# Retention's sample rows through a DRAM scratch, spreads by transposes, and a re-paced first norm

## The chip, the cores and the metric

The kernel runs on one core of a Trainium2 chip. Its engines are TensorE (PE, with PEld for its weight loads), VectorE (DVE), ScalarE (ACT), GpSimd (POOL) and SyncE (SP), and its loads and stores run on 16 DMA engines. The metric is the device time of one execution in microseconds. A profiled execution also gives a span, from the first to the last instruction.

## The reference

One layer of a hybrid decoder step, in float32: 256 prompt tokens and 8 sample tokens (one new token for each of 8 sequences), model width 2048.

```python
xn = rmsnorm(x, norm1_g)
proj = xn @ w_in                      # 2048 x 6144: [u | v | q | k | v | g]
# mixer A: gated MLP, 8 groups, position mixing within 128 tokens
# mixer B: retention, 8 heads of 128, decay gamma_h = 1 - 2^(-5-h):
scores = einsum('bihd,bjhd->bhij', qc, kc) * decay_mask
new_state = state * chunk_decay + einsum('bjhd,bjhe->bhde', kc * k_decay, vc)
# per-head GroupNorm, swish gate
h = x + concat(out_a, out_b) @ w_out
h = h + cross_attend(rmsnorm(h, norm2_g), mk, mv, w_cq, w_co)   # 256 memory tokens, 4 heads
h = h + square(relu(rmsnorm(h, norm3_g) @ w_ff1)) @ w_ff2       # 2048 -> 8192 -> 2048
y = rmsnorm(h, final_norm_g)
```

For a sample token b retention is one step of the recurrence: the head's 128 x 128 state of that sequence becomes gamma * state + k_b v_b, and the output is q_b times the new state. The states, the memory keys and values and the normalized v rows are outputs too.

## The kernel before

Activations lie transposed, 128 features on the partitions and 264 tokens along the row: the 8 sample tokens in columns 0 to 7, then two blocks of 128 (`TOK`). Every large product is made in three matmuls: operands are split into a rounded high part and a remainder (`wh` and `wl`, `xh` and `xl`), and hi x hi, hi x lo and lo x hi are added up in PSUM (lines 155 to 157).

**The weight stream.** A weight chunk is 256 x 512, 512 KB. `emit_dma` loads it on SP's queue into one of five raw buffers `w`, six chunks ahead; `emit_hi` casts it on ACT (L1040) and `emit_lo` subtracts on DVE (L1048), three and two chunks ahead, into four buffers each. A group is 8 chunks and gives 512 output columns in four PSUM banks. Five banks (`mm`) serve these groups; three more (`ms`) serve everything small.

**The order is written by hand.** The kernel is emitted in one Python loop over the chunks, and each engine runs its own instructions in the order of emission. A group's chunk has four points, one after every six matmuls. At each point `run_point` advances work that is due: every `chain` generator that is due goes on to its next `yield`, then one of the `tasks` that are due does (at most one per point, and one per lane), then stores that are due are issued on SP. `yield n` means due again in n points; a bare `yield` means 3. So yields set where on each engine's list an instruction stands. A group's eviction is emitted at its last point.

**The first norm.** The input projection runs on the raw x times its gain, and the norm's factor is applied at the eviction. `square_x`, a chain that starts at the end of the first group (v), squares x on ACT in four pieces (L333, L337), adds them on DVE (L339 to L342), sums over the partitions with matmuls against `ones` (`column`, L273), takes the root on GpSimd and spreads the factor over all partitions (`spread`, L281, called in `tables`). `tables` multiplies it into the rotary tables. Then v's first group is multiplied by it (L349). The second group, q, needs the tables at its eviction: `ev_rope` copies each bank on ACT (`z`, L529) and multiplies it on DVE (`ra`, L530), and only then is the bank free.

**Spread.** The root comes out as a column, one value per token on the partitions. A matmul with the column, broadcast to 128 columns, as the stationary operand and the identity as the moving one gives a tile in which every partition holds the row of factors. It is used for the first norm, the memory's norm, the norms before cross-attention and before the MLP, and twice at the end.

**Retention.** Eight heads run as tasks on two lanes beside the projection groups (even heads on r0, odd on r1). For the sample tokens a head transposes 8 columns of k and of q (L99, out `tp[0:8, 256:512]`), splits them into `kq` (L596 on ACT, L597 on DVE), and for each sample token b a matmul with a selector column `sel` spreads its k and q rows over all partitions in PSUM (`bc`, L626). DVE then updates the state of b (L629) and multiplies it by q with a sum along the row (L632, out `rjk`, sum in `rs_t`). Tokens go in four pairs per head. `rs_t` is transposed into the output tile `rp`, normalized, and written back over v. State tiles and many other tiles share 26 slots of one pool; `load_state` loads a head's state and decay table two heads ahead. The gate (`ev_g`) multiplies by the result.

**Stores** stand in a queue by due time, and the first one that is not due holds those behind it.

Of the kernel before, what the change touches and what calls it, by code (L numbers as in the profile page):

```python
# [30 lines left out]
def build(tc, I, O):  # L31
    cst = tc.tile_pool(name="cst", bufs=1)
    wpool = tc.tile_pool(name="wpool", bufs=1)
    spool = tc.tile_pool(name="spool", bufs=1)
    tpool = tc.tile_pool(name="tpool", bufs=1)
    psum = tc.tile_pool(name="psum", bufs=1, space=bass.MemoryType.PSUM)
    with cst as cst, wpool as wpool, spool as spool, tpool as tpool, psum as psum:
        with tc.manual_schedule():
            _emit(tc, cst, wpool, spool, tpool, psum, I, O)


def _emit(tc, cst, wpool, spool, tpool, psum, I, O):
    nc = tc.nc
# [40 lines left out]
    gcol = cst.tile([128, 96], F32, name="gcol")  # L84
    ones = cst.tile([128, 256], F32, name="ones")
    neghalf = cst.tile([128, 4], F32, name="neghalf")
# [116 lines left out]
    def store(dst, src, delay=10):  # L203
        stores.append((now[0] + delay, dst, src))

# [7 lines left out]
    def run_point():  # L213
        for e in list(chains):
            if e[0] <= now[0] and not advance(e):
                chains.remove(e)
        used = set()
        for e in tasks:
            if e[2] is not None:
                if e[2] in used:  # L220
                    continue
                used.add(e[2])
            if e[0] <= now[0]:
                if not advance(e):
                    tasks.remove(e)
                break
        while stores and stores[0][0] <= now[0]:
            _, dst, src = stores.popleft()
            sp.dma_start(out=dst, in_=src)

# [6 lines left out]
    class Stats:  # L237
# [40 lines left out]
        def spread(self, out, tok=TOK):  # L278
            ps = misc([128, self.n], "rsb")
            for i, (c0, n) in enumerate(tok):  # L280
                pe.matmul(ps[:, c0:c0 + n], lhsT=self.col[:, i:i + 1].broadcast_to([128, 128]),  # L281
                          rhs=ident[:, 0:n], start=True, stop=True)
            if out is None:
                return ps
            act.copy(out, ps[:])
# [15 lines left out]
    open_pool("rpool")  # L301
    dve.memset(ones[:, 0:128], 1.0 / 2048)
    dve.memset(ones[:, 128:256], 1.0)
    dve.memset(neghalf[:], -0.5)
# [12 lines left out]
    def keep_warm(count):  # L317
        for _ in range(count):
            wm = bank([128, 256], "wm")
            pe.matmul(wm[:], lhsT=ones[:, 128:256], rhs=ones[:], start=True, stop=True)  # L320

# [9 lines left out]
    def square_x():  # L331
        a = slot([128, 4, T], "sqa")
        act.activation(a[:], hT[0][:], AF.Square)  # L333
        yield
        for s in range(1, 4):
            b = slot([128, 4, T], "sqb")
            act.activation(b[:], hT[s][:], AF.Square)  # L337
            yield 2
            dve.tensor_tensor(out=a[:], in0=a[:], in1=b[:], op=ALU.add)  # L339
            yield  # L340
        dve.tensor_tensor(out=a[:, 0:2, :], in0=a[:, 0:2, :], in1=a[:, 2:4, :], op=ALU.add)
        dve.tensor_tensor(out=st1.acc[:], in0=a[:, 0, :], in1=a[:, 1, :], op=ALU.add)  # L342
        yield 3
        st1.column()
        yield 4
        tables()
        for m in R4:
            vt = S["v"][0][:, m, :]
            dve.tensor_tensor(out=vt, in0=vt, in1=S["rs1"][:], op=ALU.mult)  # L349
# [6 lines left out]
    def clear():  # L356
        zt = half("zt")
        dve.memset(zt[:], 0.0)
        S["kq"] = [S["rpool"].tile([128, 256], F32R, name="kq", tag="kq", bufs=2) for _ in range(2)]
        yield  # L360
        for i in range(2):
            act.copy(S["kq"][i][:], zt[:, 0:256])
        dve.tensor_tensor(out=sel[:], in0=ident[:, 0:8], in1=ident[:, 32:40], op=ALU.add)
        act.activation(halfgn[:], gcol[:, G_GN:G_GN + 8], AF.Copy, scale=0.5)
# [125 lines left out]

    mix = {}

# [27 lines left out]
    def ev_rope(which, g):  # L520
        def ev(ps):
            o = slot([128, 4, T], which)
            S.setdefault(which, []).append(o)
            tab = S["tab"]
            ta = 0 if which == "q" else 2
            z = [t264("z") for _ in R4]
            a = [t264("ra") for _ in R4]
            for m in R4:
                act.copy(z[m][:], ps[m][:])  # L529
                dve.tensor_tensor(out=a[m][:], in0=ps[m][:], in1=tab[:, ta, :], op=ALU.mult)  # L530

            def gen():
                for m in R4:
                    for lo, hi in ((0, 64), (64, 0)):
                        gp.tensor_tensor(out=o[lo:lo + 64, m, :], in0=z[m][hi:hi + 64, :],
                                         in1=tab[hi:hi + 64, ta + 1, :], op=ALU.mult)
                yield 10
                for m in R4:
                    dve.tensor_tensor(out=o[:, m, :], in0=o[:, m, :], in1=a[m][:], op=ALU.add)
                if which == "k" and g == 0:  # L540
                    retentions(0)
            chain(gen())
            if which == "q" and g == 0:
                chain(clear(), 12)
        return ev
# [22 lines left out]
    def load_state(h):  # L568
        if h < 8:
# [4 lines left out]
            S["state"][h] = (t, d)  # L574

    def retention(h):
        g, m = h // 4, h % 4
# [3 lines left out]
        def row(name):  # L581
            return S["rpool"].tile([128, 384], F32, name=name, tag="st", bufs=4)

        kn, vn = row("kn"), row("vn")
        sm = S["rpool"].tile([128, 384], F32, name="sm", tag="sm", bufs=2)
        kq = S["kq"][h % 2]
        tp = misc([128, 512], "tp")
        for i in range(2):
            c0 = TOK[i][0]
            transpose(tp[:, i * 128:(i + 1) * 128], kt[:, c0:c0 + 128])  # L590
        for i, src in enumerate((kt, qt)):
            transpose(tp[0:8, 256 + i * 128:384 + i * 128], src[:, 0:8])
        for i in range(2):
            act.activation(kn[:, i * 128:(i + 1) * 128], tp[:, i * 128:(i + 1) * 128], AF.Copy,
                           scale=kdec[:, i * 8 + h:i * 8 + h + 1])
        act.copy(kq[0:8, :], tp[0:8, 256:512])  # L596
        dve.tensor_tensor(out=kq[32:40, :], in0=tp[0:8, 256:512], in1=kq[0:8, :].bitcast(F32), op=ALU.subtract)  # L597
        yield
        tp = misc([128, 256], "tp")
# [3 lines left out]
        act.copy(vn[:, 0:256], tp[:])  # L603
        yield
        sc = misc([128, 384], "sc")
# [4 lines left out]
        load_state(h + 2)  # L610
        yield
        pp = misc([128, 128], "pp")
# [6 lines left out]
        act.activation(st[:], st[:], AF.Copy, scale=GAMMA[h])  # L619
        yield  # L620
        rs_t = S["rpool"].tile([128, 8], F32, name="rs_t", tag="rs_t", bufs=2)
        for b0 in range(0, 8, 2):
            bc = misc([128, 2, 256], "bc")
            for j in range(2):
                b = b0 + j
                pe.matmul(bc[:, j, :], lhsT=sel[:, b:b + 1].broadcast_to([128, 128]), rhs=kq[:], start=True, stop=True)  # L626
            for j in range(2):
                b = b0 + j
                dve.scalar_tensor_tensor(out=st[:, b, :], in0=bc[:, j, 0:128], scalar=vt[:, b:b + 1],  # L629
                                         in1=st[:, b, :], op0=ALU.mult, op1=ALU.add)  # L630
                j2 = S["rpool"].tile([128, 128], F32, name="rjk", tag="rjk", bufs=1)
                dve.scalar_tensor_tensor(out=j2[:], in0=st[:, b, :], scalar=1.0, in1=bc[:, j, 128:256],  # L632
                                         op0=ALU.mult, op1=ALU.mult, accum_out=rs_t[:, b:b + 1])
            yield 2
        store(O["state_s"][h], st[:])
# [32 lines left out]
        for i, (c0, n) in enumerate(TOK):  # L668
            transpose(tp[:, c0:c0 + n], rn[0:n, i * 128:(i + 1) * 128])
        act.activation(vt, tp[:], AF.Copy, scale=halfgn[:, h:h + 1])  # L670

    def ev_g(g):
        def ev(ps):
# [3 lines left out]
            def gen():  # L677
                w = [t264("gw") for _ in R4]
                for m in R4:
                    act.activation(w[m][:], z[m][:], AF.Tanh, scale=0.5)  # L680
                yield
                for m in R4:
                    dve.scalar_tensor_tensor(out=w[m][:], in0=w[m][:], scalar=1.0, in1=z[m][:],
# [42 lines left out]
    def mem_prep():  # L726
# [15 lines left out]
        def fin():  # L742
            tok = ((0, 128), (128, 128))
            st.column(tok)
            yield 4
            S["rsmb"] = cst.tile([128, 256], F32, name="rsmb")
            st.spread(S["rsmb"][:], tok)
            S["rsm"] = st.col
# [111 lines left out]
    def ev_mk(h):  # L860
        def ev(ps):
            z = [t264("kz") for _ in R4]
            for m in R4:
                dve.tensor_tensor(out=z[m][:, 0:256], in0=ps[m][:], in1=S["rsmb"][:], op=ALU.mult)
                store(O["mem_k"][h, :, m], z[m][:, 0:256])
# [353 lines left out]
```

## Time and profile before

| | |
|---|---|
| median of 3 runs | 1600.93 us (1600.66 to 1602.39) |
| the profiled execution | 1600.87 us |
| its span | 1599.1 us |
| PE busy | 1585.5 us (99%) |
| DVE, ACT, POOL busy | 1040.9 us (65%), 751.1 us (47%), 124.1 us (8%) |
| DMA | 326.15 MB, 204 GB/s |
| granted TensorE clock | 0.999 |

In rows of the profile L155 is a line of the kernel, `acc<-xh,wh` is the tile written and those read, and a releaser behind `<-` is what ended the idle time. An f32 matmul shows as two PE records, an f32 transpose as one, and one with rounded operands as one. Busy times of matmuls overlap, since the next starts before the one ahead has drained; the distance between starts is what one costs.

### The profile page before, as it was taken

The page shows a single profiled execution, that of the slowest core. Times are in us where ns is not written, and L with a number is a line of the kernel's source. Part 1 is how long each engine was busy: PE and PEld are TensorE (multiplying, and loading weights), DVE is VectorE, ACT ScalarE, POOL GpSimd, SP SyncE. Part 2 cuts the span into 40 slices and gives each one's busy share as a digit, 9 for nine tenths or more (in the row PEclk, how much of TensorE's full clock was granted, in tenths as well). Part 3 has the DMA queues.
Part 4 walks back from the last instruction along what each step waited for, and adds up shares of the span by engine and source line. Part 5 has one row for each costly group of instructions (what it writes and reads, how often), then busy time and mean ns, then how long its engine had stood idle before and what let it go on. Part 6 is the DMA issues. An engine that isn't in the chain of part 4 may idle for free.

```text
span 1599.1 us, 31005 instructions
## 1 busy us (share of the span) xinstructions
PE 1585.5 (99%) x12608; PEld 1559.4 (98%) x12608; DVE 1040.9 (65%) x1885; ACT 751.1 (47%) x1169; POOL 124.1 (8%) x111
## 2 busy tenths in 40 slices
PE   9999999999999999999999999999999999999997
PEld 9999999999999998999999999999999999999997
DVE  6677788778658777877655555655655565565555
ACT  6455565447444444444444543534444353444443
POOL 0242022000012201010000000000000000000000
PEclk9999999999999999999999999999999999999999
DMA  8556646355578887877555555555555556555552
GB/s 291 179 208 218 217 167 198 136 196 210 188 262 287 307 301 276 294 272 250 174 183 185 183 173 186 172 190 180 177 190 172 187 172 189 180 178 187 171 188 84
DMA packets 94222, 326.15 MB, mean 204 GB/s; under 512 B 10608, under 2 KB 15728, under 8 KB 94080
## 3 DMA queue, kind: packets, MB, share of 16 engines
q1 hardware_dynamic: 94080, 324.18, 59.5%
q8 instruction: 98, 1.61, 0.4%
q14 instruction: 44, 0.36, 0.1%
HBM read 313.03 MB, written 11.11 MB: 203 GB/s over the span
## 4 chain that ended last, share of the span: by engine, by line
PE 48%; issue 46%; DVE 1%; POOL 0%; ACT 0%; POOLq 0%; DVEq 0%
PE acc L155 13%; PE acc L157 13%; PE acc L156 13%; PE acc L179 2%; PE acc L181 2%; PE acc L180 2%; PE tp L99 1%; PE qb L827 0%; PE bc L626 0%; PE spp L480 0%; PE sc L904 0%; PE op L926 0%; PE sc L903 0%; PE op L927 0%; PE pb L850 0%
## 5 line engine op out<-in xcount | busy, mean ns | idle before, releaser
L1040 ACT CAST wh<-w 128x1024 fp32r<-128x1024 f32 (+1 forms) x513 | 535.9, 1045 | 709.6 <-PE acc L156 625.4
L1048 DVE TENSOR_TENSOR wl<-w,wh 128x1024 fp32r<-128x1024 f32 (+1 forms) x513 | 628.3, 1236 | 257.2 <-ACT wh L1040 256.5
L155 PE MATMUL acc<-h2h,wh 128*128 128x264 f32 x1024 | 291.5, 285 | 0.0
L157 PE MATMUL acc<-h2h,wl 128*128 128x264 f32 x1024 | 291.1, 284 | 0.0
L156 PE MATMUL acc<-h2l,wh 128*128 128x264 f32 x1024 | 290.5, 284 | 0.0
L155 PE MATMUL acc<-rh,wh 128*128 128x264 f32 x992 | 282.2, 284 | 0.0
L157 PE MATMUL acc<-rh,wl 128*128 128x264 f32 x992 | 282.0, 284 | 0.0
L156 PE MATMUL acc<-rl,wh 128*128 128x264 f32 x992 | 281.4, 284 | 0.0
L155 PE MATMUL acc<-xh,wh 128*128 128x264 f32 x768 | 225.6, 294 | 2.8 <-DVE ra L530 2.6
L157 PE MATMUL acc<-xh,wl 128*128 128x264 f32 x768 | 219.3, 285 | 0.0
L156 PE MATMUL acc<-xl,wh 128*128 128x264 f32 x768 | 218.7, 285 | 0.0
L156 PEld LDWEIGHTS acc<-h2l,wh 128*128 128x128 f32 x1024 | 192.8, 188 | 0.0
L155 PEld LDWEIGHTS acc<-h2h,wh 128*128 128x128 f32 x1024 | 192.6, 188 | 0.0
L157 PEld LDWEIGHTS acc<-h2h,wl 128*128 128x128 f32 x1024 | 192.4, 188 | 0.0
L156 PEld LDWEIGHTS acc<-rl,wh 128*128 128x128 f32 x992 | 186.8, 188 | 0.0
L155 PEld LDWEIGHTS acc<-rh,wh 128*128 128x128 f32 x992 | 186.6, 188 | 0.0
L157 PEld LDWEIGHTS acc<-rh,wl 128*128 128x128 f32 x992 | 186.4, 188 | 0.0
L155 PEld LDWEIGHTS acc<-xh,wh 128*128 128x128 f32 x768 | 145.7, 190 | 4.9 <-DVE ra L530 3.2
L156 PEld LDWEIGHTS acc<-xl,wh 128*128 128x128 f32 x768 | 146.0, 190 | 0.2 <-DVE xl L107 0.2
L157 PEld LDWEIGHTS acc<-xh,wl 128*128 128x128 f32 x768 | 145.3, 189 | 0.0
L958 DVE TENSOR_TENSOR hT<-hT,acc 128x264 f32<-128x264 f32 x124 | 53.2, 429 | 73.2 <-PE acc L157 73.2
L95 POOL TENSOR_TENSOR msr<-msv,neghalf 128x3 f32<-128x3 f32 (+1 forms) x5 | 7.7, 1549 | 990.2 <-DVE msv L268 738.0
(253 smaller groups left out, 2777.9 us busy)
## 6 DMA issues: line engine op xcount, KB each, us to landing
w<-in_w_ff_dram SPq DMA_DIRECT2D x256, 512.0 KB, 4.1
w<-in_w_in_dram SPq DMA_DIRECT2D x95, 512.0 KB, 3.7
w<-in_w_out_dram SPq DMA_DIRECT2D x32, 512.0 KB, 4.0
w<-in_w_cq_dram SPq DMA_DIRECT2D x32, 512.0 KB, 4.2
kv<-in_kN_dram SPq DMA_DIRECT2D x32, 512.0 KB, 5.2
kv<-in_vT_dram SPq DMA_DIRECT2D x32, 512.0 KB, 4.9
w<-in_w_ck_dram SPq DMA_DIRECT2D x32, 512.0 KB, 5.6
w<-in_w_cv_dram SPq DMA_DIRECT2D x32, 512.0 KB, 4.7
```

The costliest lines, as they stand in the source:

```text
L95: gp.tensor_tensor(out=out, in0=in_, in1=neghalf[0:in_.shape[0], 0:n], op=ALU.pow)
L99: pe.transpose(out, in_, ident[0:p, 0:p])
L155: pe.matmul(ps, lhsT=a, rhs=xh, start=(i == 0), stop=False)
L156: pe.matmul(ps, lhsT=a, rhs=xl, start=False, stop=False)
L157: pe.matmul(ps, lhsT=b, rhs=xh, start=False, stop=(i == nk - 1))
L179: pe.matmul(ps, lhsT=a, rhs=hi[:, k, :], start=(kt == 0), stop=False)
L180: pe.matmul(ps, lhsT=a, rhs=lo[:, k, :], start=False, stop=False)
L181: pe.matmul(ps, lhsT=b, rhs=hi[:, k, :], start=False, stop=(kt == 15))
L958: dve.tensor_tensor(out=h[m], in0=h[m], in1=ps[m][:], op=ALU.add)
L1040: act.copy(hi[:, k, :], raws[i][:, k, :])
L1048: dve.tensor_tensor(out=lo[:, k, :], in0=raw[:, k, :], in1=hi[:, k, :].bitcast(F32), op=ALU.subtract)
```

## The change

- `sample_rows(g)`, a task once per group of four heads: copies the 8 sample columns of k and q of the four heads into one tile, transposes both (32 rows out), copies them to SBUF and stores them as 32 rows of 256 floats into a DRAM scratch `kqd{g}`.
- `rows_of(h, b0)`: a load on SP's queue of two rows (2 KB), sent to all 128 partitions, into one of four buffers `bkq`. A head asks for the first pair when it starts and for each next pair when it begins on the one before. The selector matmuls of retention, `kq` and its zeroing, split and transposes go; DVE reads `bkq` instead of PSUM and writes its throw-away product over the k half.
- Retention's yields: 2 instead of 3 between the head's first steps, 4 instead of 2 between pairs. A head waits with its start until the store of the rows has been issued.
- Stores are issued when each is due, without holding one another.
- `spread` makes transposes of the broadcast column, each 128 columns wide, the sample tokens' first so that the others overwrite what it has too much.
- `square_x` has shorter yields: squares every 2 points instead of 5, the column 6 points after the last adds instead of 3, the tables 5 points after the column instead of 4, v's products 2 points after the tables.
- `ones` has 128 columns instead of 256 and one memset fewer; the warm-up matmuls read it twice. The memory's factor moves into another pool. Cross-attention keeps its selector matmuls.

```diff
         def spread(self, out, tok=TOK):
             ps = misc([128, self.n], "rsb")
-            for i, (c0, n) in enumerate(tok):
-                pe.matmul(ps[:, c0:c0 + n], lhsT=self.col[:, i:i + 1].broadcast_to([128, 128]),
-                          rhs=ident[:, 0:n], start=True, stop=True)
+            for i, (c0, _) in reversed(list(enumerate(tok))):
+                transpose(ps[:, c0:c0 + 128], self.col[:, i:i + 1].broadcast_to([128, 128]))
...
     def square_x():
-        a = slot([128, 4, T], "sqa")
-        act.activation(a[:], hT[0][:], AF.Square)
-        yield
-        for s in range(1, 4):
-            b = slot([128, 4, T], "sqb")
+        q = []
+        for s in R4:
+            b = slot([128, 4, T], "sqa")
             act.activation(b[:], hT[s][:], AF.Square)
-            yield 2
-            dve.tensor_tensor(out=a[:], in0=a[:], in1=b[:], op=ALU.add)
-            yield
+            q.append(b)
+            yield 1
+            if s:
+                dve.tensor_tensor(out=q[0][:], in0=q[0][:], in1=q.pop()[:], op=ALU.add)
+                yield 1
+        a = q[0]
...
-        yield 3
+        yield 6
         st1.column()
-        yield 4
+        yield 5
         tables()
+        yield 2
         for m in R4:
             vt = S["v"][0][:, m, :]
             dve.tensor_tensor(out=vt, in0=vt, in1=S["rs1"][:], op=ALU.mult)
...
-                if which == "k" and g == 0:
-                    retentions(0)
+                if which == "k":
+                    defer(sample_rows(g), 2)
+                    if g == 0:
+                        retentions(0)
...
+    def sample_rows(g):
+        if g == 0:
+            S["kqd"], S["kqe"] = {}, {}
+        cols = S["rpool"].tile([128, 2, 32], F32, name="kqcol", tag="kqcol", bufs=1)
+        for i, w in enumerate("kq"):
+            act.copy(cols[:, i, :].rearrange("p (m b) -> p m b", m=4), S[w][g][:, :, 0:8])
+        yield 2
+        tp = misc([32, 2, 128], "tp")
+        for i in range(2):
+            transpose(tp[:, i, :], cols[:, i, :])
+        rows = half("kqrow")[0:32, 0:256]
+        act.copy(rows, tp[:].rearrange("p a d -> p (a d)"))
+        S["kqd"][g] = dpool.tile([32, 256], F32, name=f"kqd{g}")
+        S["kqe"][g] = store(S["kqd"][g][:], rows, 3)
+        yield
+
+    def rows_of(h, b0):
+        t = S["rpool"].tile([128, 2, 256], F32, name="bkq", tag="bkq", bufs=4)
+        r = 8 * (h % 4) + b0
+        sp.dma_start(out=t[:].rearrange("p b f -> p (b f)"),
+                     in_=S["kqd"][h // 4][r:r + 2, :].rearrange("b f -> (b f)").partition_broadcast(128))
+        return t
...
     def retention(h):
...
+        while g not in S["kqe"] or not S["kqe"][g][3]:
+            yield 2
+        yield 2
+        ahead = rows_of(h, 0)
...
-        for i, src in enumerate((kt, qt)):
-            transpose(tp[0:8, 256 + i * 128:384 + i * 128], src[:, 0:8])
...
-        act.copy(kq[0:8, :], tp[0:8, 256:512])
-        dve.tensor_tensor(out=kq[32:40, :], in0=tp[0:8, 256:512], in1=kq[0:8, :].bitcast(F32), op=ALU.subtract)
-        yield
+        yield 2
...
         for b0 in range(0, 8, 2):
-            bc = misc([128, 2, 256], "bc")
-            for j in range(2):
-                b = b0 + j
-                pe.matmul(bc[:, j, :], lhsT=sel[:, b:b + 1].broadcast_to([128, 128]), rhs=kq[:], start=True, stop=True)
+            bc = ahead
+            if b0 < 6:
+                ahead = rows_of(h, b0 + 2)
             for j in range(2):
                 b = b0 + j
                 dve.scalar_tensor_tensor(out=st[:, b, :], in0=bc[:, j, 0:128], scalar=vt[:, b:b + 1],
                                          in1=st[:, b, :], op0=ALU.mult, op1=ALU.add)
-                j2 = S["rpool"].tile([128, 128], F32, name="rjk", tag="rjk", bufs=1)
-                dve.scalar_tensor_tensor(out=j2[:], in0=st[:, b, :], scalar=1.0, in1=bc[:, j, 128:256],
+                dve.scalar_tensor_tensor(out=bc[:, j, 0:128], in0=st[:, b, :], scalar=1.0, in1=bc[:, j, 128:256],
                                          op0=ALU.mult, op1=ALU.mult, accum_out=rs_t[:, b:b + 1])
-            yield 2
+            yield 4
```

More of the change, by code (lines that the diff above doesn't have):

```diff
@@ L36, in build, with _emit @@
     psum = tc.tile_pool(name="psum", bufs=1, space=bass.MemoryType.PSUM)
-    with cst as cst, wpool as wpool, spool as spool, tpool as tpool, psum as psum:
+    dpool = tc.tile_pool(name="dpool", bufs=1, space=bass.MemoryType.DRAM)
+    with cst as cst, wpool as wpool, spool as spool, tpool as tpool, psum as psum, dpool as dpool:
         with tc.manual_schedule():
-            _emit(tc, cst, wpool, spool, tpool, psum, I, O)
-def _emit(tc, cst, wpool, spool, tpool, psum, I, O):
+            _emit(tc, cst, wpool, spool, tpool, psum, dpool, I, O)
+def _emit(tc, cst, wpool, spool, tpool, psum, dpool, I, O):
     nc = tc.nc
@@ L84, in _emit @@
     gcol = cst.tile([128, 96], F32, name="gcol")
-    ones = cst.tile([128, 256], F32, name="ones")
+    ones = cst.tile([128, 128], F32, name="ones")
     neghalf = cst.tile([128, 4], F32, name="neghalf")
@@ L203, in store @@
     def store(dst, src, delay=10):
-        stores.append((now[0] + delay, dst, src))
+        e = [now[0] + delay, dst, src, False]
+        stores.append(e)
+        return e
     def advance(e):
@@ L226, in run_point @@
                 break
-        while stores and stores[0][0] <= now[0]:
-            _, dst, src = stores.popleft()
-            sp.dma_start(out=dst, in_=src)
+        for e in [e for e in stores if e[0] <= now[0]]:
+            sp.dma_start(out=e[1], in_=e[2])
+            e[3] = True
+            stores.remove(e)
     def flush():
@@ L301, in _emit @@
     open_pool("rpool")
-    dve.memset(ones[:, 0:128], 1.0 / 2048)
-    dve.memset(ones[:, 128:256], 1.0)
+    dve.memset(ones[:], 1.0 / 2048)
     dve.memset(neghalf[:], -0.5)
@@ L318, in keep_warm @@
         for _ in range(count):
-            wm = bank([128, 256], "wm")
-            pe.matmul(wm[:], lhsT=ones[:, 128:256], rhs=ones[:], start=True, stop=True)
+            wm = bank([128, 2, 128], "wm")
+            pe.matmul(wm[:], lhsT=ones[:], rhs=ones[:].unsqueeze(1).broadcast_to([128, 2, 128]), start=True, stop=True)
     keep_warm(NWARM)
@@ L356, in clear @@
     def clear():
-        zt = half("zt")
-        dve.memset(zt[:], 0.0)
-        S["kq"] = [S["rpool"].tile([128, 256], F32R, name="kq", tag="kq", bufs=2) for _ in range(2)]
         yield
-        for i in range(2):
-            act.copy(S["kq"][i][:], zt[:, 0:256])
         dve.tensor_tensor(out=sel[:], in0=ident[:, 0:8], in1=ident[:, 32:40], op=ALU.add)
@@ L489, in spatial @@
         yield
-    mix = {}
+    mix, done = {}, set()
     def split4(dst, src):
@@ L582, in row @@
             return S["rpool"].tile([128, 384], F32, name=name, tag="st", bufs=4)
+        while g not in S["kqe"] or not S["kqe"][g][3]:
+            yield 2
+        yield 2
+        ahead = rows_of(h, 0)
         kn, vn = row("kn"), row("vn")
         sm = S["rpool"].tile([128, 384], F32, name="sm", tag="sm", bufs=2)
-        kq = S["kq"][h % 2]
-        tp = misc([128, 512], "tp")
+        tp = misc([128, 256], "tp")
         for i in range(2):
@@ L603, in retention @@
         act.copy(vn[:, 0:256], tp[:])
-        yield
+        yield 2
         sc = misc([128, 384], "sc")
@@ L610, in retention @@
         load_state(h + 2)
-        yield
+        yield 2
         pp = misc([128, 128], "pp")
@@ L619, in retention @@
         act.activation(st[:], st[:], AF.Copy, scale=GAMMA[h])
-        yield
+        yield 2
         rs_t = S["rpool"].tile([128, 8], F32, name="rs_t", tag="rs_t", bufs=2)
         for b0 in range(0, 8, 2):
-            bc = misc([128, 2, 256], "bc")
-            for j in range(2):
-                b = b0 + j
-                pe.matmul(bc[:, j, :], lhsT=sel[:, b:b + 1].broadcast_to([128, 128]), rhs=kq[:], start=True, stop=True)
+            bc = ahead
+            if b0 < 6:
+                ahead = rows_of(h, b0 + 2)
             for j in range(2):
@@ L670, in retention @@
         act.activation(vt, tp[:], AF.Copy, scale=halfgn[:, h:h + 1])
+        done.add(h)
     def ev_g(g):
@@ L681, in gen @@
                 yield
+                assert done.issuperset(range(4 * g, 4 * g + 4))
                 for m in R4:
@@ L745, in fin @@
             yield 4
-            S["rsmb"] = cst.tile([128, 256], F32, name="rsmb")
-            st.spread(S["rsmb"][:], tok)
+            r = tpool.tile([128, T], F32, name="rstd", tag="rstd", bufs=2)
+            st.spread(r[:, 0:256], tok)
+            S["rsmb"] = r
             S["rsm"] = st.col
@@ L863, in ev @@
             for m in R4:
-                dve.tensor_tensor(out=z[m][:, 0:256], in0=ps[m][:], in1=S["rsmb"][:], op=ALU.mult)
+                dve.tensor_tensor(out=z[m][:, 0:256], in0=ps[m][:], in1=S["rsmb"][:, 0:256], op=ALU.mult)
                 store(O["mem_k"][h, :, m], z[m][:, 0:256])
```

## The prediction

> **What bounds the kernel now.** I read the page first (busy time, the groups, the DMA issues), then the list of who waited for whom on PE, then the timeline around each edited line, then the table of stretches.
>
> ```profile
> span 1599.1 us, 31005 instructions
> PE 1585.5 (99%) x12608; PEld 1559.4 (98%) x12608; DVE 1040.9 (65%) x1885; ACT 751.1 (47%) x1169; POOL 124.1 (8%) x111
> L1040 ACT CAST wh<-w 128x1024 fp32r<-128x1024 f32 (+1 forms) x513 | 535.9, 1045 | 709.6 <-PE acc L156 625.4
> ```
>
> PE is busy 99% of the span. The weight cast, the step that could starve it, spends its own idle time waiting for PE (625.4 of 709.6 us), so the weights are there before PE wants them. PE's waits confirm it:
>
> ```profile
> PE acc L155 <- DVE ra L530: 2.6, 3, 1.8
> PE wm L320 <- DVE neghalf L304: 1.2, 1, 1.2
> ...
> PE rp L638 <- DVE rjk L632: 0.3, 1, 0.3
> ...
> PE rp L99 <- DVE rjk L632: 0.2, 1, 0.2
> ```
>
> Nothing is left to win but PE instructions and the 1.8 us wait. An instruction taken from PE comes off the end one for one, unless a new wait takes its place. PE starts a main matmul every 0.12 us (91.36 to 91.48 below; its 0.28 us of busy time is pipelined), so removed work is costed by shifted starts and not by busy time. One point of the hand-written schedule is six matmuls, 0.73 us.
>
> **Part 1, the selector matmuls of retention (gone).**
>
> ```profile
> L626 PE MATMUL bc<-kq,sel 128*128 128x256 f32 x64 | 12.7, 280 | 0.0
> ...
> 101.87 0.28 PE L157 MATMUL acc<-xh,wl 128*128 128x264 f32 x1
> 101.99 0.40 PE L626 MATMUL bc<-kq,sel 128*128 128x256 f32 x2
> 102.22 0.28 PE L155 MATMUL acc<-xh,wh 128*128 128x264 f32 x1
> ```
>
> The first row's 12.7 us is overlapped busy time. In the timeline a pair occupies PE from 101.99 to 102.22, 0.23 us. 32 pairs: **-7.4 us**. Retention's vector work stays, reading SBUF where it read PSUM.
>
> **Part 2, the small transposes.** Each head transposed 8 columns of k and of q; now two transposes per group of four heads do it.
>
> ```profile
> 91.36 0.29 PE L157 MATMUL acc<-xh,wl 128*128 128x264 f32 x1
> 91.48 0.49 PE L99 MATMUL tp<-cmat,k 128*128 128x128 f32 x3
> 91.81 0.27 PE L99 MATMUL tp<-cmat,q 128*8 128x128 f32 x1
> ...
> 92.05 0.28 PE L156 MATMUL acc<-xl,wh 128*128 128x264 f32 x1
> ```
>
> From 91.36 to 92.05 is 0.69 us with two ordinary slots (0.24) in it, so four transposes cost 0.45 us, 0.11 each. 16 go and 4 come: 12 x 0.11 = **-1.3 us**. The cast and the subtraction into kq go; two small copies per group come on ACT, which is 47% busy: nothing.
>
> **Part 3, the factors spread by transposes.** A spread of three was six PE records (each f32 matmul is two); it becomes three transposes.
>
> ```profile
> 51.41 0.28 PE L157 MATMUL acc<-xh,wl 128*128 128x264 f32 x1
> 51.53 0.73 PE L281 MATMUL rsb<-cmat,msr 128*128 128x128 f32 x6
> 52.11 0.37 PE L155 MATMUL acc<-xh,wh 128*128 128x264 f32 x1
> 52.32 0.29 PE L156 MATMUL acc<-xl,wh 128*128 128x264 f32 x1
> ...
> 1589.24 1.50 PE L281 MATMUL rsb<-cmat,msr 128*128 128x128 f32 x12 [0.32 <-POOL msr L95]
> ```
>
> 0.91 us less two slots is 0.67; three transposes are 0.34. Three such spreads save 0.33 each, the memory's spread of two about 0.2: -1.2. The two at the end lie bare, 1.50 us for both. Six transposes take some 0.7, the vector products need only the first half and GpSimd's the second, so 0.3 to 0.8 of it; I take 0.4. Together **-1.6 us**. On this the Trainium skill, "TensorE: Matmul & The Clock Gate", Terms, says that transpose mode is four times faster for FP32; by that a spread of three would fall from 0.67 to 0.17 and the sum would be 0.7 us lower, while the 0.11 us per transpose above is about half of an f32 matmul's 0.22, and I keep that.
>
> **Part 4, the denser first norm.**
>
> ```profile
> 32.65 1.08 ACT L333 ACTIVATE sqa<-hT 128x1056 f32<-128x1056 f32 x1
> ...
> 44.66 0.43 DVE L342 TENSOR_TENSOR sq<-sqa 128x264 f32<-128x264 f32 x1
> ...
> 53.87 2.58 DVE L349 TENSOR_TENSOR vt<-vt,rstd 128x264 f32<-128x264 f32 x4
> 56.38 1.77 DVE L1048 TENSOR_TENSOR wl<-w,wh 128x1024 fp32r<-128x1024 f32 x1
> 58.07 1.44 DVE L530 TENSOR_TENSOR ra<-acc,tab 128x264 f32<-128x264 f32 x4
> ...
> 56.47 0.28 PE L157 MATMUL acc<-xh,wl 128*128 128x264 f32 x1
> 58.55 0.39 PE L155 MATMUL acc<-xh,wh 128*128 128x264 f32 x1 [1.79 <-DVE ra L530]
> ```
>
> The rotary products of q's first group free PSUM. They run at 58.07, behind v's four products (2.58 us) and a cast (1.77 us), and PE starts at 58.55 where 56.59 was due: 1.96 us lost. By the yields the tables came 25 points after the first square and now come 18 after it, 7 x 0.73 = 5 us earlier; v's products start two points later, 3.6 us earlier than now. They end near 53, before the last banks of q are full, and the wait goes: **-1.9 us**. The price is density: four squares of 1.08 us and two casts (1.05 each) now stand together on ACT, and the last adds on DVE end near 42, where the column's matmuls are due at 13 points, 32.65 + 9.5 = 42.1. A wait of up to 0.4 us may show there; casts have two chunks (5.8 us) of cover. One memset fewer at the start: nothing, since the first loads decide there.
>
> **Part 5, sample rows through DRAM (the unknown).** 32 loads of 256 KB, each a 2 KB row sent to 128 partitions, and two small stores join SP's queue. DVE's products, which waited for PE, now wait for a landing.
>
> ```profile
> w<-in_w_in_dram SPq DMA_DIRECT2D x95, 512.0 KB, 3.7
> ...
> dec<-in_c_dec_dram SPq DMA_DIRECT2D x8, 128.0 KB, 5.7
> out_state_p_dram<-so SPq DMA_DIRECT2D x8, 64.0 KB, 3.2
> bbc<-in_sgu_b_dram SPq DMA_DIRECT2D x1, 512.0 KB, 6.6
> ...
> SPq L1034 <- DVE wl L1048: 1091.2, 445, 7.7
> ...
> 100.00:280.00 180.00, 178.75 (x1455) 175.20 (x1454) 141.72 (x388) 104.83 (x248) 42.90 (x38) 1.00 0.59 198
> ```
>
> A row is asked for four points before use, 2.9 us, plus whatever SP runs ahead. SP's only large wait is for the cast that frees a raw weight buffer, and that cast is emitted a chunk before the weight load it releases, so SP is normally ahead, by up to a chunk: lead 2.9 to 5.8 us. The landing lies between 3.7 (a plain load of twice the size) and 6.6 us (a broadcast in a burst of four loads). So a row comes between 2.1 us early and 3.7 us late. DVE idles 38.3 us of the stretch 100 to 280; with some 9 us of PE time gone 29 are left, 0.9 us for each of 32 pairs. From -0.5 us (the two rjk waits, gone because rs_t now has six points instead of four) to (3.7 - 0.9) x 32 = +90 us. I take the plain load's 3.7, the nearest row (same queue, same stretch, not in a burst): rows arrive in time or nearly so, and what remains is a late eviction at some of the six group ends in the stretch: **+0.8 us** (the size of the second and third ra waits, 2.6 - 1.8), less 0.5: **+0.3**.
>
> The Trainium skill, "DMA: Bandwidth & Descriptors", Anatomy of one DMA, fits a DMA as 2.0 us plus bytes at 436 GB/s. Worked out from it, an estimate: 2.6 us for 256 KB, always in time, and the sum would be 0.8 us lower. The 3.2 us of the 64 KB store and 5.7 us of the 128 KB dec load are above it, so I keep the rows' own numbers.
>
> Behind each row load in SP's queue stand the weight loads. The group's first row load also waits until the store of the two rows has landed (3.2 us), which it was given six points for; a later one waits for its buffer, four loads old and freed one or more steps before. A weight is loaded six chunks ahead and cast three ahead of its use, so three chunks, 8.7 us, less the 3.7 of landing: 5 us of cover at each such stop. Data: 8.4 MB in 180 us are 47 GB/s on 198 at a DMA share of 0.59, so to about 0.73: not a bound. Heads get slower, 8 + 16 points to their state store instead of 12 + 8; two lanes still end the last head some 80 points before the output projection needs the pool, and states stay longer in their slots by about 17 points, which costs only if a load waits for a state's store.
>
> **Sum.** -7.4 - 1.3 - 1.6 - 1.9 + 0.3 = -11.9 us. The profiled execution took 1600.87 us (1.8 outside the span); the median of the runs is 1600.93, so the same base. 1600.9 - 11.9 = **1589.0 us**, 0.74% faster. Some 0.2%, 3.2 us, is what a measurement can tell from no change.
>
> **Rivals.**
> *Some rows late.* In the points where two lanes run pairs, a row's buffer is free only four points earlier and SP's lead is gone: 5.7 - 2.9 = 2.8 us late there and at evictions. A few such PE waits, 3 to 8 us in all: 1592 to 1597. For: the ra waits show that evictions have little slack. Against: pairs of one lane now come every four points instead of two, so DVE's work is more even.
> *Slower: all rows late.* DVE stands behind a landing at every pair, its casts and evictions queue behind, PE pays. Decides at 0.9 + (11.9 + 3.2)/32 = 1.4 us late per pair on average. With 6.6 landing and a lead of 4.4 they are 2.2 late: (2.2 - 0.9) x 32 = 42 us, 1631. Against: the weight loads of the same stretch land in 3.7.
> *The selector slots were cover.* If PE reaches the evictions sooner and waits there for DVE (141.72 of 180 busy), the 9 us of parts 1 and 2 come back as ra and z waits: 1598. Against: DVE has 29 us left after the cut.
>
> **How the numbers follow.** Forecast 0.60 (its own range 1587 to 1592, from the ends of parts 3, 4 and 5); below 1587 0.03; some rows late 0.24; slots were cover 0.07; all rows late 0.06. The range 1586.5 to 1596 leaves out the last two and the end of the second. Faster 0.03 + 0.60 + 0.24 and a little of the cover case, 0.88; same 0.06; slower 0.06.
>
> **What would show it.** No bc records on PE, 4 transposes with a 32-row output, spreads of 3 records. PE with no ra wait near 58. In the stretch 100 to 280 as many main matmuls in some 9 us less. DVE's state products waiting for bkq landings by under 0.9 us each; if PE's waits name state, kn, z or ra after 100 us, the rows are late. SP waits on landings of kqd twice. Wrong if PE's waits grow beyond some 4 us.

## The result and the profile after

The changed kernel takes 1588.4 us (median of 4 runs, 1588.26 to 1588.74) against 1601.6 us for the kernel before beside it; the ratio is 0.9917, with a 95% interval from 0.9904 to 0.993. The forecast was 1589.0. The kernel before scatters by 2 to 3.5 us from run to run (1600.66 to 1604.21 over 21 runs) and the changed one by half a microsecond, so below I compare the spans of profiled executions where a microsecond matters: 1599.1 before, 1587.0 after, 12.1 us less where the sum said 11.9. By the medians it is 13.2 us less, since the profiled execution of the kernel before is one of its shorter ones.

The page of the changed kernel, its busy times and the cast's group:

```profile
span 1587.0 us, 30814 instructions
PE 1573.1 (99%) x12515; PEld 1546.7 (97%) x12515; DVE 1038.5 (65%) x1875; ACT 748.3 (47%) x1165; POOL 122.0 (8%) x111
L1064 ACT CAST wh<-w 128x1024 fp32r<-128x1024 f32 (+1 forms) x513 | 535.8, 1045 | 696.9 <-PE acc L157 620.4
```

PE is still the bound, and the casts still wait for it. Who waited for whom on PE in the changed kernel:

```profile
PE acc L156 <- DVE vt L557: 1.2, 1, 1.2
PE wm L322 <- DVE neghalf L306: 1.1, 1, 1.1
...
PE rp L100 <- DVE bkq L653: 0.3, 1, 0.3
```

The ra wait is gone entirely, its second and third occurrence too, and one new wait of size has come, for v's second eviction; short waits in the first 30 us differ from profile to profile. Where the time went is read from the evictions, which mark how far PE is. Columns are the number, then the shortest, median and longest duration in ns, then first and last start in us. First the kernel before, then the changed one:

```profile
L390 DVE TENSOR_TENSOR z<-acc,rstd x24: 410/433/435, 195.1 to 336.6; 128x264 f32<-128x264 f32 x24
L864 DVE TENSOR_TENSOR kz<-acc,rsmb x16: 402/413/425, 553.7 to 715.0; 128x256 f32<-128x256 f32 x16
L556 DVE TENSOR_TENSOR vt<-acc,rstd x4: 422/424/429, 166.5 to 167.5; 128x264 f32<-128x264 f32 x4
```

```profile
L389 DVE TENSOR_TENSOR z<-acc,rstd x24: 410/433/434, 186.4 to 325.9; 128x264 f32<-128x264 f32 x24
L888 DVE TENSOR_TENSOR kz<-acc,rstd x16: 402/415/425, 542.4 to 703.7; 128x256 f32<-128x256 f32 x16
L557 DVE TENSOR_TENSOR vt<-acc,rstd x4: 421/422/425, 161.0 to 162.0; 128x264 f32<-128x264 f32 x4
```

The lead over the kernel before is 5.5 us at v's second group, 8.7 at the first z, 10.7 at the last, 11.3 while the memory's keys are made (`kz`), and 12.1 at the end. It grows only where something was taken away: the wait near 58, the matmuls of retention, the spreads, and the end.

### The profile page after: what moved, and what is told of

It is laid out like the page before. It is cut to its first block, busy times and chain, and to the rows that moved or that the text cites. A ratio compares the mean times of both kernels' runs of the same rounds, so it can differ in the third digit from the quotient of the medians.

```text
span 1587.0 us, 30814 instructions
## 1 busy us (share of the span) xinstructions
PE 1573.1 (99%) x12515; PEld 1546.7 (97%) x12515; DVE 1038.5 (65%) x1875; ACT 748.3 (47%) x1165; POOL 122.0 (8%) x111
## 4 chain that ended last, share of the span: by engine, by line
PE 49%; issue 47%; DVE 2%; DMA 1%; POOL 0%; SPq 0%; DVEq 0%; ACT 0%; POOLq 0%
PE acc L156 13%; PE acc L158 13%; PE acc L157 13%; PE acc L180 2%; PE acc L182 2%; PE acc L181 2%; PE tp L100 1%; DVE wl L1072 1%; DMA bkq<-kqd 1%; PE qb L851 0%; DMA w<-in_w_in_dram 0%; DVE state L651 0%; PE spp L479 0%; DVE bkq L653 0%; PE op L950 0%
```

## The experiments

**Each part alone.** Three kernels take the change apart: the kernel before with the new `square_x`; the kernel before with the new `spread`; and the changed kernel with both put back, which leaves the rows through DRAM. The lines show the spread as the third kernel puts it back; the second has the same lines the other way round.

```diff
 # e1: before, with square_x of the change     # e2: before, with spread of the change
 # e3: the changed kernel, with these two functions of before
-            for i, (c0, _) in reversed(list(enumerate(tok))):
-                transpose(ps[:, c0:c0 + 128], self.col[:, i:i + 1].broadcast_to([128, 128]))
+            for i, (c0, n) in enumerate(tok):
+                pe.matmul(ps[:, c0:c0 + n], lhsT=self.col[:, i:i + 1].broadcast_to([128, 128]),
+                          rhs=ident[:, 0:n], start=True, stop=True)
```

> The kernel before with the denser first norm alone. Theory (the wait of PE at the end of q's first group is what the norm buys): 1.9 us below before, no ra wait near 58, retention as before. Rival (the wait only moves to the next group's end): within 0.5 us of before, with ra waits of 1 to 2 us after 60.

> The kernel before with the spreads by transposes alone. Theory: 1.6 us below before (0.33 for each of three spreads of three, 0.2 for the memory's, 0.4 at the end), and since the tables come 0.33 us earlier the ra wait near 58 may shrink by as much. Rival (the middle spreads are slots that PE gives back to waits): only the 0.4 us at the end.

> The changed kernel with the first norm's yields and the matmul spreads of before put back: rows through DRAM and the fewer transposes alone. Theory: 7.4 + 1.3 - 0.3 = 8.4 us below before, with the ra wait near 58 still there (1.8 us). Rival (the selector slots were cover for DVE): 5 us or less below before, with eviction waits between 100 and 280 of 3 us and more.

The spans are 1597.2, 1597.8 and 1590.5 us: 1.9, 1.3 and 8.6 us below before, against 1.9, 1.6 and 8.4 expected. They add up to 11.8 of the 12.1. Tenths are uncertain, because the starts differ: ACT's first eviction of v begins at 29.36 in the kernel before, at 29.56, 29.78 and 29.54 in these three and at 29.40 in the changed one. The spreads' 1.3 us is therefore nearer to 1.7. In run times the parts are less sharp (ratios 0.9982 [0.9973, 0.9991], 0.9987 [0.9978, 0.9996], 0.9939 [0.9926, 0.9951]), because of the scatter of the kernel before. PE's waits in the first of them:

```profile
PE acc L155 <- DVE ra L532: 0.8, 2, 0.6
```

and in the third:

```profile
PE acc L156 <- DVE ra L528: 1.8, 1, 1.8
...
PE acc L156 <- DVE vt L556: 0.7, 1, 0.7
```

The 1.8 us wait belongs to the norm alone and does not move to the next group; the two small ra waits in retention go with the rows; the vt wait comes with the rows. All three rivals fall.

**The new wait.** In the changed kernel's list of DVE and SP work by time, a pair waits for its row, and the work behind it arrives late at v's eviction:

```profile
148.84 0.43 SPq L596 DMA_DIRECT2D bkq<-kqd  x1
...
155.05 0.35 DVE L651 SCALAR_TENSOR_TENSOR state<-bkq,vt,state 128x128 f32<-128x128 f32 x1 [1.65 <-DMA bkq<-kqd]
...
161.02 1.44 DVE L557 TENSOR_TENSOR vt<-acc,rstd 128x264 f32<-128x264 f32 x4
...
161.50 0.39 PE L156 MATMUL acc<-xh,wh 128*128 128x264 f32 x1 [1.24 <-DVE vt L557]
```

The row for the product at 155.05 is the one issued at 148.84, between four other transfers that SP issues from 147.90 to 149.91; it landed at 155.03, 6.2 us after its issue. DVE has no idle time between 155.05 and 161.02, so what it lost to the row it still owed at the eviction. To test that, each row was asked for two pairs ahead, every second one into a buffer of another pool:

```diff
-        ahead = rows_of(h, 0)
+        ahead = [rows_of(h, 0), rows_of(h, 2)]
...
-            bc = ahead
-            if b0 < 6:
-                ahead = rows_of(h, b0 + 2)
+            bc = ahead.pop(0)
+            if b0 < 4:
+                ahead.append(rows_of(h, b0 + 4))
```

> The changed kernel with rows asked for two pairs ahead instead of one (8 points, 5.8 us, before use; every second row in a buffer of another pool). Theory (DVE's 1.65 us wait for a row at 155 is what makes v's eviction and PE late by 1.24 us at 161): no DVE wait for bkq, no PE wait for vt, 1.2 us below the changed kernel, 1587.2. Rival (the eviction is late because DVE has too much to do there): the vt wait stays near 1 us and the time within 0.4 us of the changed kernel.

1587.4 us (1587.31 to 1587.73), span 1585.5: 1.0 us below the changed kernel by the medians, 1.5 by the spans. Neither the bkq wait of DVE nor the vt wait of PE is left. Without the late row there is no wait, so the row is a cause of it; the next experiment shows a second one. This version beats both kernels.

**The selector matmuls put back.** Beside the rows, 64 matmuls with nobody to read them:

```diff
+            xb = misc([128, 2, 256], "xb")
+            for j in range(2):
+                pe.matmul(xb[:, j, :], lhsT=sel[:, b0 + j:b0 + j + 1].broadcast_to([128, 128]),
+                          rhs=A[0][0][:, j, 0:256], start=True, stop=True)
             bc = ahead
```

> The changed kernel with retention's 64 selector matmuls of 128x256 put back beside the rows; nothing reads what they write. Theory (PE slots are the end's time one for one, 0.23 us a pair): 7.4 us above the changed kernel, 1595.8. Rival (the slots were cover, PE would only wait for DVE in their place): 4 us or less above it.

1593.8 us (1593.61 to 1593.92), 5.4 us above the changed kernel: between the two. One of its pairs by time:

```profile
101.64 0.28 PE L158 MATMUL acc<-xh,wl 128*128 128x264 f32 x1
101.76 0.39 PE L648 MATMUL xb<-xh,sel 128*128 128x256 f32 x2
101.99 0.28 PE L156 MATMUL acc<-xh,wh 128*128 128x264 f32 x1
```

A pair occupies the same 0.23 us as before, 7.4 for all, and the vt wait (1.2) and rp wait (0.3) are absent here. So 1.5 of the missing 2.0 us are waits that the freed slots had uncovered; the other 0.5 I cannot place (by the spans of the two profiles, which lie 4.8 us apart, it is 1.1). DVE waited for the same pair's row as in the changed kernel (1.49 us, at 156.31), and PE did not wait for v's eviction: a late row costs PE time only where PE itself comes early enough.

**How much lead the rows need.** First the rows asked for in the step that uses them:

```diff
-        ahead = rows_of(h, 0)
...
-            bc = ahead
-            if b0 < 6:
-                ahead = rows_of(h, b0 + 2)
+            bc = rows_of(h, b0)
```

> The changed kernel with each pair's rows asked for in the same step that uses them, so that the four points (2.9 us) of lead go and only SP's own lead is left. Theory (a row lands 5.4 us after its issue, DVE waits in order, 0.9 us a pair is free and the rest comes out of PE): DVE waits for bkq of 40 to 110 us in all and 10 to 50 us above the changed kernel. Rival (SP runs far enough ahead that the asking point does not matter): DVE waits of under 10 us and within 2 us of the changed kernel.

1608.7 us (1607.86 to 1611.83), 20.3 above the changed kernel and slower than the kernel before (ratio 1.0045, 1.003 to 1.006). DVE's waits between 100 and 280, and PE's:

```profile
DVE state L648 <- DMA bkq<-kqd: 24.6, 16, 4.3
```

```profile
PE rp L100 <- DVE bkq L650: 5.0, 3, 4.1
PE acc L156 <- DVE vt L557: 4.8, 1, 4.8
PE acc L156 <- DVE ra L529: 4.1, 2, 2.4
PE acc L156 <- DVE z L389: 1.2, 1, 1.2
```

The rival falls. The time is inside the theory's range, but not by its reckoning. DVE waited 24.6 us, not 40 or more, at 16 of the 32 pairs: half of the rows came in time by SP's own lead. That is 0.77 us a pair, less than the 0.9 that I had called free, and PE still waited 15.1 us. The rest of the 20 us is clock (last section).

Then two points between pairs instead of four, and after that the same with more room ahead of a head's sum:

```diff
 # e7, and e8 on top of it
-            yield 4
+            yield 2
         store(O["state_s"][h], st[:])
-        yield 2
+        yield 6
```

> The changed kernel with 2 points between pairs, as before the change, instead of 4: the lead is 1.5 us and a head's four pairs stand closer on DVE. Theory (lead plus SP's lead is 4.4 us at most against 5.4 of landing): DVE waits for bkq of 10 to 40 us in all, PE waits of some 1 to 8 us more, 1589 to 1596. Rival (SP's lead alone covers the landing): no change, within 0.6 us.

> The kernel with 2 points between pairs, and now 6 points instead of 2 between a head's last pair and the matmuls that read its sum. Theory (there PE did not wait for rows but came to the sum too soon: 4.7 us of rp waits, DVE's waits for bkq only 1.3 us): rp waits under 1 us, what is left is the ra wait near 107, 1588.5 to 1591. Rival (rows come too late at that pace and DVE is behind in any case): the waits move to evictions and the time stays above 1593.

The first took 1595.4 us (1594.81 to 1598.57), 7.0 above the changed kernel: in the theory's range, but DVE's waits for rows were only 1.3 us in its profile, not 10 to 40, and PE waited at the heads' sums:

```profile
PE rp L100 <- DVE bkq L653: 4.7, 3, 2.6
PE acc L156 <- DVE ra L529: 1.7, 1, 1.7
```

So I blamed the sum's place, and that fell. With six points it took 1594.5 us (1592.02 to 1595.97), no better than by its scatter, with the waits elsewhere, as the rival had it:

```profile
PE acc L156 <- DVE ra L529: 3.3, 1, 3.3
PE rp L100 <- DVE bkq L653: 1.4, 1, 1.4
PE tp L100 <- ACT vn L422: 1.1, 1, 1.1
```

In this profile DVE waited 10.1 us for rows, in the one before 1.3. With one profile of each kernel it is not shown whether the six points or the run decides that; PE was held up in either case. What part is lateness and what part the denser order of DVE's work stays open. The four points are worth 6 to 7 us.

**The order inside the norm.** The new norm alone, with v's products right behind the tables:

```diff
         tables()
-        yield 2
         for m in R4:
```

> The kernel before with the denser first norm alone, but without the two points between the tables and v's products. Theory (7 points earlier is what matters; v's products end near 51 in either order): as with the two points, no ra wait near 58, span near 1597.2. Rival (v's products must stand behind a cast, or they delay it): a wait of 0.5 us or more at q's end and a span above 1597.7.

1598.9 us (median of 10 runs, 1598.61 to 1599.37), span 1597.5, no ra wait near 58: as with the two points (median 1599.2). The seven points of density carry the gain, and the two points behind the tables do nothing that can be measured.

**The scatter of the kernel before.** The new norm alone, in its two forms, gave 20 of 21 runs between 1598.38 and 1599.37, while the kernel before has many runs near 1600.8 and near 1602.7, the latter mostly with a mean clock of 0.997 instead of 0.998 or 0.999. It was run twice more for a profile of the upper kind.

> The kernel before, unchanged, for a second profile: its runs fall into two clusters, near 1600.8 and near 1602.7, and the runs of the kernels without the wait at 58 do not. Theory (PE's wait of 1.96 us there now and then lowers the granted clock for the microseconds behind it): in a profile of the upper cluster the clock between 55 and 70 is below 0.9, in one of the lower cluster 1.00 as in the profile shown. Rival (the 2 us come from elsewhere, the start or the end): a profile of the upper cluster has 1.00 there and the loss in another stretch.

> As the run ahead of it: the kernel before once more, for a profile in the cluster that the other one missed. Theory: clock below 0.9 between 55 and 70 if it lands near 1602.7, 1.00 if near 1600.8. Rival: no difference there.

Both profiled executions fell to the lower kind (spans 1599.3 and 1599.0; all runs 1600.61 to 1602.93). So the theory was not tested. The last section shows stretches of 3.41 us at half clock, 1.7 us lost each, and one of them would fit the distance of the two kinds. That the wait at 58 brings it about is not shown: the rows alone keep that wait (1.8 us), and their five runs lie within 1.0 us of each other.

## Why the prediction was right, point by point

**The selector matmuls.** Right in size: 0.23 us a pair, measured again above. The rows alone gave 8.6 us where 7.4 + 1.3 - 0.3 was due. "One for one" was a little too simple: 1.5 us of the freed slots turned into waits, which the sum had booked in part under the rows.

**The transposes.** The changed kernel's first spread by time:

```profile
46.34 0.28 PE L158 MATMUL acc<-xh,wl 128*128 128x264 f32 x1
46.46 0.49 PE L100 MATMUL rsb<-cmat,msr 128*128 128x128 f32 x3
46.71 0.37 PE L156 MATMUL acc<-xh,wh 128*128 128x264 f32 x1
46.91 0.28 PE L157 MATMUL acc<-xl,wh 128*128 128x264 f32 x1
...
1577.46 0.87 PE L100 MATMUL rsb<-cmat,msr 128*128 128x128 f32 x6 [0.32 <-POOL msr L96]
```

From 46.34 to 46.91 less two slots is 0.33 us for three; 0.34 was said. By the factor of four of the Trainium skill, "TensorE: Matmul & The Clock Gate", Terms, it would have been 0.17, by estimate. At the end both spreads take 0.87 instead of 1.50, 0.63 less. What came of it is less: from DVE's last addition into `hT` (1586.12 before, 1574.34 after) to the end of the span the kernel gained 0.3 us, where 0.4 was taken.

**The first norm.** Right in mechanism and size; its price did not come. By time in the changed kernel:

```profile
41.48 0.43 DVE L345 TENSOR_TENSOR sq<-sqa 128x264 f32<-128x264 f32 x1
...
42.17 0.83 PE L277 MATMUL msq<-ones,sq 128*128 128x128 f32 x6
...
49.69 1.46 DVE L353 TENSOR_TENSOR vt<-vt,rstd 128x264 f32<-128x264 f32 x4
...
54.09 0.43 DVE L529 TENSOR_TENSOR ra<-acc,tab 128x264 f32<-128x264 f32 x1 [0.67 <-ACT z L528]
```

The last add ends at 41.91 and the column starts at 42.17, as close as reckoned, without a wait. The rotary products follow PE now: they wait for `z`, not for v's products.

**The rows.** The net was right (+0.3 foreseen; PE's ra and rp waits between 100 and 280 were 1.3 us before, vt and rp are 1.5 now), and two of its steps were not, so that it was luck in part. I took the plain weight load's landing, 3.7 us, as nearest. The rows' own, shortest, median and longest:

```profile
DMA to landing us min/median/max: 3.4/5.4/7.3
```

5.4 is near the burst loads that I set aside. It is far from the 2.6 us, an estimate, that I worked out from "DMA: Bandwidth & Descriptors", Anatomy of one DMA, of the Trainium skill; that fit is for transfers issued from GpSimd, and the rows are issued on SP. Most rows still came in time because SP runs further ahead of DVE than I allowed. I had a lead of 2.9 to 5.8 us; by the trace a row was issued 5.0 to 14.1 us before the product that used it, 7.8 by the median. With no asked lead it was still issued 4.4 us (median) before DVE was ready for it, and half of the rows came in time. A landing taken 1.7 us too short and a lead taken some 2 us or more too short cancelled. And the threshold, 0.9 us a pair free, was an average: the rows asked for on use stayed below it and cost 20 us. A wait is paid for where an eviction stands close behind it (of 1.65 us on DVE 1.24 reached PE), however idle DVE is elsewhere. So "all rows late" would have decided far sooner than at 1.4 us a pair.

**The other rivals.** Some rows late: two, 1.65 and 0.66 us on DVE, of which 1.2 us reached PE, not 3 to 8. Slots were cover: for 1.5 us. DMA share went to 0.75 in the stretch 100 to 280 (0.73 was said).

## What to carry to other kernels

Where one engine is busy 99%, cost its removed instructions by the distance between starts, then look for the two or three places where a neighbour's work stands just ahead of an eviction; those, not a neighbour's mean idle time, decide what a late transfer costs. A broadcast that a saturated TensorE makes can be a DMA's work if the row is asked for more than one landing ahead by the loaded queue's own time, and if the engine that consumes it keeps its even pace.

## What the runs showed of the hardware

**After a PE wait of 2.4 us or more the granted clock was halved for 3.4 or 6.8 us.** Stretches of the kernel with rows on use; the last three columns are granted clock, DMA share and GB/s:

```profile
100.00:110.00 10.00, 8.32 (x67) 8.06 (x66) 6.91 (x14) 6.25 (x12) 6.80 (x8) 1.00 0.52 167
...
133.60:137.00 3.40, 0.98 (x9) 0.77 (x7) 1.98 (x5) 3.40 (x13) 0.00 (x0) 1.00 0.83 235
137.00:140.40 3.40, 3.40 (x18) 3.40 (x17) 2.44 (x6) 1.26 (x3) 1.61 (x3) 0.50 0.82 264
140.40:150.00 9.60, 9.60 (x78) 9.36 (x77) 8.50 (x16) 5.16 (x9) 7.63 (x7) 1.00 0.74 272
171.20:177.90 6.70, 5.97 (x27) 5.97 (x28) 5.89 (x19) 2.31 (x7) 1.69 (x1) 0.50 0.53 160
178.00:190.00 12.00, 12.00 (x100) 11.79 (x99) 4.67 (x11) 6.32 (x19) 0.85 (x1) 1.00 0.85 289
215.60:218.90 3.30, 3.28 (x16) 3.28 (x17) 3.23 (x11) 0.00 (x0) 0.00 (x0) 0.50 0.73 246
219.00:230.00 11.00, 11.00 (x94) 10.89 (x93) 9.13 (x25) 7.20 (x25) 3.42 (x3) 1.00 0.60 213
```

The wait of 1.7 us in the first left the clock at 1.00. With those of 2.4, 4.8 and 4.1 us, which end at 136.40, 171.93 and 215.62, it fell to 0.50; by the trace's record of the clock this lasted 3.41, 6.83 and 3.41 us (from 137.00, 171.14 and 215.51). Half of that is lost: 1.7 + 3.4 + 1.7 = 6.8 us. In the two kernels with two points between pairs a wait of 2.55 and one of 3.28 us were each followed by 3.41 us at 0.50; in all these profiles no wait of 1.9 us or less was. So the price was 1.7 or 3.4 us per wait, not a share of the wait. With 13.6 us more of waits than in the changed kernel (15.1 against 1.5) the 6.8 us make 20.4, a little more than the 19.6 us between the spans (1606.6 and 1587.0); part of the second stretch falls into its wait. "TensorE: Matmul & The Clock Gate" of the Trainium skill, Part 1, has the clock halve after an idle window of about 3.4 us. The trace agrees that it halves, and the shorter stretches are as long as that window; but 2.4 us of wait were enough here.

**DVE slows beside GpSimd when both of its inputs are in SBUF.** v's four products took 2.58 us before, at 53.87, and take 1.46 now, at 49.69. GpSimd's rotary products decide it, here in the kernel before and then in the changed one:

```profile
54.48 10.20 POOL L535 TENSOR_TENSOR q<-z,tab 64x264 f32<-64x264 f32 x8 [3.63 <-ACT z L529]
```

```profile
54.19 9.41 POOL L534 TENSOR_TENSOR q<-z,tab 64x264 f32<-64x264 f32 x8 [9.13 <-ACT z L528]
```

Before, the first two of v's products took 0.43 us each, and the two that start after GpSimd's first product 0.99 and 0.98. The ra products beside GpSimd read PSUM and keep their 0.43 us. The change put retention's products on the wrong side of this, and I had booked the move from PSUM to SBUF at nothing. Before, then after:

```profile
L629 DVE SCALAR_TENSOR_TENSOR state<-bc,vt,state x64: 332/347/352, 102.5 to 246.5; 128x128 f32<-128x128 f32 x64
```

```profile
L651 DVE SCALAR_TENSOR_TENSOR state<-bkq,vt,state x64: 339/347/875, 101.8 to 243.9; 128x128 f32<-128x128 f32 x64
```

The median is the same, the longest 875 ns instead of 352. By the trace, the four of the 64 that overlap a GpSimd product in the changed kernel are the four long ones, 840 to 875 ns; before, 14 overlapped one and none was long. "SBUF — State Buffer", SBUF: two separate sides, of the Trainium skill states the rule: a DVE instruction with two SBUF inputs and a GpSimd instruction that reads SBUF lock each other out. The trace agrees that DVE slows; that one engine stands still for the other is not shown.
